# Exchanging the halves of a rotated state by a second matrix product instead of by a transfer, in a State-space and convolution layer

## The chip, the cores and the metric

The kernel runs on one core of a Trainium2 chip. The metric is the device time of one execution in microseconds (us): the median of several executions, and, for everything read from a profile, one profiled execution. The core has five engines that work side by side, each strictly in its own order: TensorE (PE in the profile; its weight loads are listed as PEld), VectorE (DVE), ScalarE (ACT), GpSimd (POOL) and SyncE (SP), which here does nothing but start transfers (DMA).

## The reference

One decoder layer is computed for a prompt of 1024 tokens and for 8 sample tokens that carry on from a stored state, so 1032 columns in all. The model width is 1024. What matters here:

```
xn = rmsnorm(x);  z = xn @ w_in
u, cv, cg = z[:512], z[512:1024], z[1024:1536]; gates = sigmoid(z[1536:])
h_t = a * h_(t-1) + B u_t            # complex, 32 groups of 16 channels, 64 states each
y   = Re(C h) + d * u                # the state-space branch
ya  = (gelu(y) @ w_glu)[:1024] * sigmoid((gelu(y) @ w_glu)[1024:])
c   = silu(layernorm(dwconv31(cv * sigmoid(cg))));  yb = c @ w_pw
x   = x + (gates[:1024] * ya + gates[1024:] * yb) @ w_out
x   = x + (silu(g) * v) @ w_ff_out   # g, v from rmsnorm(x) @ w_ff_in, width 2816
y   = rmsnorm(x)
```

The outputs are y for both groups of tokens, the new complex state and the new rows of the convolution's buffer.

## The kernel before

Channels lie on the 128 partitions and tokens on the free axis. Large products run in fp16 with the weights in two parts (`wh` and `wl`, three products for each block, tile `mm`, L594), 344 or 384 columns at a time; ScalarE and VectorE make the weight parts (L561, L565) with a scale `wsc` (L501) that VectorE computes. The program runs through these stages: load and normalise x and project u (0 to about 92 us in the profile), the products of the convolution's two inputs and of gate a (to about 304), the gated products of the state-space branch (`gyp`, to 437), the layer norm of the convolution (to 448), gate b and the pointwise product (to 538), the output product (to 672), and the feed-forward part (to the end).

The state-space recurrence, called the chain here, lies inside the second stage. It is done in 8 blocks of 4 groups. The 1024 prompt tokens are cut into 128 pieces of 8 tokens, and for each group the 8 x 16 inputs of a piece lie on the 128 partitions, so the tile `U` has 128 columns of pieces for each group, beside 8 columns for the sample tokens. The state lies on the 128 partitions too, 64 real parts above 64 imaginary parts. For each block:

- `s1` (L355): fp32 products `px = E . U` give what each piece adds to the state. ScalarE copies them to `X` in SBUF (L358) and the 8 sample columns to `xs` (L359). Two transfers (L342, L343) write the tile `Y`, which is `X` with its two halves of 64 partitions exchanged, since a rotation needs the real part beside the imaginary part.
- `s2`: VectorE multiplies `X` by cosines (L366) and `Y` by sines (L367), adds them (L368), and runs four scans along the 128 pieces (L371). What is scanned is then real for each row. Two further transfers write the exchanged result back into `X`.
- `s3`: VectorE multiplies by cosine and sine again (L381, L382) and subtracts into `H` (L385), shifted by one piece; `hf` (L386) keeps the last column as the final state. GpSimd sets the first column of `H` and copies the stored state of the sample tokens behind it (L384, L387). TensorE forms `py = Q . H + M . U` (L394, L395), 8 fp32 products of 136 columns. ScalarE and VectorE apply the gelu (L396 to L400), and transfers write `gy` to DRAM (`gd`, L828), from where it is read back as `gyt` with channels on the partitions.

The coefficients are made on the way: `coef_w` makes the matrices `E` (tile `pe`, L301) and, for two blocks together, `kv`; `coef_m` sends `kv` through DRAM (`kvd`, L312) and reads it back as the matrix `M` (L316); `coef_p` makes cosines and sines `pc` for two blocks and spreads them by transfers into `cosi` (L337, L338); `coef_q` makes `Q`. The products `px`, `pe`, `py` and `pf` share one pool of PSUM with two buffers (tag `ms`), so a third of them can start only when the first has been read out.

The loop over t takes 10 steps: step t does `s1` of block t, `s2` of block t-1 and `s3` of block t-2. The order of the instructions on each engine isn't the order of the code: a scheduler simulates the program with its own costs and writes one list for each engine, and `hp()` gives some transfers a higher priority. VectorE also computes the depthwise convolution of 31 taps (L898), which fills its time from about 180 to 430 us, and the statistics of its layer norm: TensorE sums them (`pst`, L1007) and spreads them over the partitions (`prb`, L1021).

Of the kernel before, what the change touches and what calls it, by code (L numbers as in the profile page):

```python
# [36 lines left out]
class S5:  # L37
# [207 lines left out]
    def prep_c(self):  # L245
# [39 lines left out]

    def coef_w(self, m):
        nc, V, A, T = self.nc, self.nc.vector, self.nc.scalar, self.nc.tensor
        kv = self.t([P, 8, 16], "^kv", bufs=1)
        for h in range(2):
            b = 2 * m + h  # L290
            gs = slice(4 * b, 4 * b + 4)
            W = self.t([P, 4, 8, 16], "^W", bufs=2)
# [4 lines left out]
            E = self.t([P, 4, P], "^E", bufs=2)
            for q in range(2):
                pe = self.ps.tile([P, 512], F32, name="pe", tag="ms")
                for g in range(2):  # L300
                    T.matmul(pe[:, 144 * g:144 * g + 144], W[:, 2 * q + g], self.IC[:, 2 * q + g],  # L301
                             start=True, stop=True)
# [1 line left out]
                A.copy(E[:, 2 * q:2 * q + 2], pv[:, :, :P])
# [13 lines left out]
    def coef_p(self, m):  # L318
# [12 lines left out]
        pv = pc.rearrange("p s (b i) x y -> p s b (i x y)", i=2)  # L331
        for h in range(2):
            b = 2 * m + h
            t = self.t([P, 2, 4, P], "^cosi", bufs=2)
            for hi_ in range(2):
                d = t[:, :, 2 * hi_:2 * hi_ + 2].rearrange("p s i n -> p s (i n)")
                SY.dma_start(d[0:64], pv[64 * hi_:64 * hi_ + 64, 0:2, h])  # L337
                SY.dma_start(d[64:128], pv[64 * hi_:64 * hi_ + 64, 0:3:2, h])  # L338
            self.cosi[b] = t
# [5 lines left out]
    def s1(self, b, U):  # L345
        A, T = self.nc.scalar, self.nc.tensor
        E = self.E.pop(b)
        Xf = self.t([P, 4, 136], "X", tag="XY", bufs=6)
        Y = self.t([P, 4, 136], "Y", tag="XY", bufs=6)[:, :, :P]
        X = Xf[:, :, :P]  # L350
        self.st[b] = (X, Y, U, Xf)
        for h in range(2):
            px = self.ps.tile([P, 512], F32, name="px", tag="ms")
            for g in range(2):
                T.matmul(px[:, g * 136:g * 136 + 136], E[:, 2 * h + g], U[:, 2 * h + g, 0:136],  # L355
                         start=True, stop=True)
# [1 line left out]
            A.copy(X[:, 2 * h:2 * h + 2], pv[:, :, 8:136])  # L358
            A.copy(self.xs[:, 4 * b + 2 * h:4 * b + 2 * h + 2], pv[:, :, 0:8])  # L359
        self.swap(Y, X)  # L360

    def s2(self, b):
# [3 lines left out]
        V.tensor_tensor(X, X, co, MUL)  # L366
# [5 lines left out]
        self.swap(X, Y)  # L372

    def s3(self, b, gy_dma):
        nc, V, A, T = self.nc, self.nc.vector, self.nc.scalar, self.nc.tensor
# [9 lines left out]
        V.tensor_tensor(H[:, :, 1:128], Y[:, :, 0:127], X[:, :, 0:127], SUB)  # L385
        V.tensor_tensor(self.hf[:, gs], Y[:, :, 127], X[:, :, 127], SUB)  # L386
        nc.gpsimd.tensor_copy(H[:, :, 128:136], self.h0[:, 0, :, gs].rearrange("p s g -> p g s"))  # L387
        gy = self.t([P, 4, 136], "gy", bufs=1)
        Qf = Q.rearrange("p g k c -> p g (k c)")
        for h in range(2):  # L390
            py = self.ps.tile([P, 512], F32, name="py", tag="ms")
            for g in range(2):
                o = py[:, g * 136:g * 136 + 136]
                T.matmul(o, Qf[:, 2 * h + g], H[:, 2 * h + g], start=True, stop=False)  # L394
                T.matmul(o, M[:, 4 * (b % 2) + 2 * h + g], U[:, 2 * h + g, 8:144], start=False, stop=True)  # L395
            A.copy(Xf[:, 2 * h:2 * h + 2].rearrange("p g n -> p (g n)"), py[:, :272])  # L396
# [6 lines left out]
    def finish(self, rep, imp, res, ims):  # L403
        nc, V, A, T = self.nc, self.nc.vector, self.nc.scalar, self.nc.tensor
        ps = self.ps.tile([P, 512], F32, name="pf", tag="ms")
        T.transpose(ps[:G, :P], self.hf, self.ident)
# [1042 lines left out]
```

## Time and profile before

| what | us |
|---|---|
| median of 3 executions | 1368.21 (1366.9 to 1368.58) |
| the profiled execution | 1366.18 |
| its span, from first to last instruction | 1364.1 |
| TensorE busy with products | 1263.1 (93%) |
| VectorE busy | 1036.5 (76%) |
| ScalarE busy | 621.6 (46%) |
| GpSimd busy | 102.8 (8%) |
| mean clock granted to TensorE | 0.975 |

The page of the profile gives busy shares over the whole span, in which the stage of the chain is less than a fifth. So for this change the views with a window count: how busy each engine was in a stretch, who waited for whom there, the chain of work that ended last, and the list of instructions in order of time. In a list, the number in brackets behind an instruction is the idle time of its engine ahead of it, and what ended it; "issue" is a wait for which the profile shows no releaser. In the views by groups, "x64" is a count and the number behind "busy" is the mean time of one instruction in ns; instructions of one engine overlap, so the distance of two starts is shorter than one duration. An fp32 product stands in the list as two records.

### The profile page before, as it was taken

What the parts mean: (1) busy time and instruction counts of PE and PEld (TensorE: products, weight loads), DVE (VectorE), ACT (ScalarE), POOL (GpSimd) and SP (SyncE); (2) the same over time, 40 slices, a digit from 0 to 9 for tenths busy, and PEclk for the clock granted to TensorE, in tenths of its full rate; (3) what the DMA queues carried; (4) which work ended last, traced back from release to release, by engine and by line L of the source; (5) the groups of instructions that cost most, each with busy time, mean ns of one, the idle gap of its engine ahead of it and who ended that gap; (6) DMA issues with size and microseconds to landing.
All of it is one profiled execution on the core that took longest, in us unless ns stands there. A gap on an engine that the chain in (4) does not pass through costs nothing.

```text
span 1364.1 us, 25399 instructions
## 1 busy us (share of the span) xinstructions
PE 1263.1 (93%) x10083; PEld 1001.7 (73%) x10083; DVE 1036.5 (76%) x2402; ACT 621.6 (46%) x1118; POOL 102.8 (8%) x198
## 2 busy tenths in 40 slices
PE   3898797999998999799979999999999999999996
PEld 2776565666666666578658888888888888888884
DVE  5976788989997744768897857776785777678758
ACT  5843433453333545744354534444453544445522
POOL 5000012001110100000000000000000000000100
PEclk9899898999999999999979999999999999999998
DMA  6445665341122123410011121112112111221203
GB/s 190 130 97 120 135 113 119 81 127 50 48 62 63 30 82 98 135 32 1 17 41 46 40 78 48 40 55 68 50 39 78 48 39 55 68 58 32 77 18 125
DMA packets 169632, 96.66 MB, mean 71 GB/s; under 512 B 12927, under 2 KB 165643, under 8 KB 169513
## 3 DMA queue, kind: packets, MB, share of 16 engines
q1 hardware_dynamic: 168109, 92.44, 24.8%
q0 software_dynamic: 896, 1.63, 0.6%
q8 instruction: 79, 1.29, 0.4%
q10 hardware_dynamic: 507, 0.97, 0.3%
q14 instruction: 41, 0.33, 0.1%
HBM read 76.72 MB, written 9.65 MB: 63 GB/s over the span
## 4 chain that ended last, share of the span: by engine, by line
PE 51%; DVE 26%; issue 9%; DMA 8%; ACT 4%; POOL 1%; SPq 1%; DVEq 0%; ACTq 0%; POOLq 0%
PE q L1291 18%; PE q L1370 12%; PE mm L594 10%; PE q L1177 5%; DMA wr<-in_w_ff_in_dram 5%; DVE acc L898 4%; PE pu L734 2%; DVE ws L1249 2%; DVE wl L565 2%; DVE tb L898 1%; DMA Y<-X 1%; POOL sv L521 1%; ACT ws L1248 1%; DVE g L1270 1%; DVE mh L609 1%
## 5 line engine op out<-in xcount | busy, mean ns | idle before, releaser
L1291 PE MATMUL q<-xs,ws 128*128 128x258 f16 (+2 forms) x3696 | 422.6, 275 | 18.7 <-DVE xs L1225 6.7
L1291 PEld LDWEIGHTS <-ws 128*128 128x128 f16 x3696 | 358.4, 98 | 81.7 <-issue 24.6
L594 PEld LDWEIGHTS <-wh 128*128 128x128 f16 x1728 | 169.5, 98 | 86.2 <-issue 5.1
L594 PE MATMUL mm<-xn,wh 128*128 128x344 f16 (+2 forms) x1152 | 203.8, 311 | 1.9 <-ACT ut L746 1.1
L1370 PE MATMUL q<-hp,wh 128*128 128x258 f16 x1280 | 193.5, 272 | 0.0
L521 POOL PARTITION_ALL_REDUCE sv<-wss x110 | 71.0, 646 | 936.0 <-ACT wh L516 510.7
L1370 PEld LDWEIGHTS <-wh 128*128 128x128 f16 x1280 | 124.0, 97 | 18.1
L561 ACT ACTIVATE wh<-wr,wsc 128x512 f16<-128x512 f32 (+1 forms) x76 | 70.0, 922 | 126.9 <-DVE wsc L501 122.6
L1370 PE MATMUL q<-hp,wl 128*128 128x258 f16 x640 | 122.5, 273 | 0.0
L594 PE MATMUL mm<-xn,wl 128*128 128x344 f16 (+2 forms) x576 | 118.0, 312 | 0.0
L594 PEld LDWEIGHTS <-wl 128*128 128x128 f16 x864 | 85.2, 99 | 41.3 <-issue 0.3
L516 ACT ACTIVATE wh<-wr 128x512 bf16<-128x512 f32 (+1 forms) x78 | 65.0, 833 | 107.6 <-PE q L1370 44.6
L516 ACT ACTIVATE junkw<-wr 128x1024 bf16<-128x1024 f32 x52 | 54.8, 1054 | 109.2 <-DMA wr<-in_w_ff_in_dram 101.6
L565 DVE SCALAR_TENSOR_TENSOR wl<-wr,wsc,wh 128x512 f16<-128x512 f32 (+1 forms) x76 | 75.9, 999 | 22.6 <-ACT wh L561 22.4
L1374 DVE SCALAR_TENSOR_TENSOR x<-q,inv,x 128x516 f32<-128x516 f32 x80 | 59.9, 750 | 35.8 <-PE q L1370 35.6
L1177 PE MATMUL q<-mh,wo 128*128 128x258 f16 x672 | 80.0, 275 | 7.5 <-ACT mh L608 4.2
L1249 DVE SCALAR_TENSOR_TENSOR ws<-sw,wsc,ws 128x512 f16<-128x512 f32 x88 | 64.7, 744 | 19.4 <-ACT ws L1248 18.4
L1177 PEld LDWEIGHTS <-wo 128*128 128x128 f16 x672 | 64.3, 96 | 19.9 <-issue 7.6
L1248 ACT ACTIVATE ws<-sw,wsc 128x512 f16<-128x512 f32 x88 | 62.3, 715 | 28.9 <-PE q L1291 28.8
L1370 PEld LDWEIGHTS <-wl 128*128 128x128 f16 x640 | 61.9, 97 | 9.0
L594 PE MATMUL mm<-gyp,wh 128*128 128x344 f16 x384 | 66.6, 309 | 1.4 <-DVE mg L971 0.8
L1249 DVE SCALAR_TENSOR_TENSOR ws<-wr,wsc,ws 128x512 f16<-128x512 f32 x66 | 48.7, 744 | 17.9 <-ACT ws L1248 17.6
(404 smaller groups left out, 1852.8 us busy)
## 6 DMA issues: line engine op xcount, KB each, us to landing
wr<-in_w_ff_in_dram SPq DMA_DIRECT2D x44, 512.0 KB
wr<-in_w_in_dram SPq DMA_DIRECT2D x28, 512.0 KB
wr<-in_w_ff_out_dram SPq DMA_DIRECT2D x44, 256.0 KB
xt<-in_x_prompt_dram SPq DMA_DIRECT2D x8, 512.0 KB
cosi<-pc SPq DMA_DIRECT2D x32, 128.0 KB
wr<-in_w_glu_dram SPq DMA_DIRECT2D x16, 256.0 KB
wr<-in_w_out_dram SPq DMA_DIRECT2D x8, 512.0 KB
xc<-in_x_prompt_dram SPq DMA_DIRECT2D x8, 512.0 KB
```

The source lines that it names most:

```text
L516: A.activation(junk, src, AF.Square, accum_out=o)
L521: GP.partition_all_reduce(v, ss, P, RMAX)
L561: A.mul(hi, raw, s)
L565: V.scalar_tensor_tensor(lo[:, sl], raw[:, sl], s, hi[:, sl], MUL, SUB)
L594: T.matmul(pt[:, c, :b - a], ww[:, k], aa[:, a:b], start=(k == 0 and i == 0), stop=(k == n - 1 and i == 2))
L898: V.scalar_tensor_tensor(o[:, q:], x[:, 0:HT - q], w[q], o[:, q:], MUL, ADD)
L1177: T.matmul(o, wo[m][u][:, k], cset(mh[k][v], j), start=(k == 0 and q == 0), stop=(k == 7 and q == 2))
L1248: A.mul(w[:, 0], src, s)
L1249: V.scalar_tensor_tensor(w[:, 1], src, s, w[:, 0], MUL, SUB)
L1291: T.matmul(o[:, z, :w_], w[:, u, k * P:(k + 1) * P], xs[k][i][:, v, c, a:b], start=(k == 0 and q == 0), stop=(k == 3 and q == 2))
L1370: T.matmul(pt[:, z, :258], w[u][:, k], hid[k][v][:, c0:c0 + 258], start=(k == 0 and q == 0), stop=(k == blocks[b] - 1 and q == 2))
L1374: V.scalar_tensor_tensor(x, pt[:, :, :258], inv, x, MUL, ADD)
```

## The change

The exchange of halves is no longer done by transfers.

- `E` gets 192 columns, the last 64 a repeat of the first 64. The product with columns 0 to 127 gives the added state, and a second product with columns 64 to 191 gives the same with its halves exchanged. `s1` so has 8 products of 128 columns in two PSUM tiles, and no copy to SBUF; `s2` multiplies straight from PSUM.
- The second exchange is moved into a coefficient: `Qs` is `Q` with its halves exchanged, by two transfers for each block. `H` has two parts, the scanned result times cosine and times sine (written by L385 of the new kernel, twice), and `py` is `Q . H[0] + Qs . H[1] + M . U`. The subtraction is gone. ScalarE copies `hf` (two parts now) and the stored state into `H`.
- The sample tokens' part of `E . U` is made by 4 products of 8 columns for each block, beside `py`.
- The final state takes four products in `finish` instead of a transpose.
- `coef_w` works block by block, `coef_c` (the spreading of cosines) is split off and works block by block too, blocks 0 and 1 are prepared ahead of the loop, `U` is loaded one block ahead, and the loop has 9 steps, with `s1` and `s2` of a block in the same step and `s3` one step later.
- The tiles under tag `XY` have 4 buffers instead of 6, those of `U` 3 instead of 4; the sample columns in `U` and `gy` change places with the prompt's.

```diff
     def coef_q(self, b):
         Q = self.t([P, 4, 8, 16], "^Q", bufs=2)
         self.build(Q, self.C[0], self.C[1], self.D1, self.D2, slice(4 * b, 4 * b + 4))
-        self.Q[b] = Q
-
-    def coef_w(self, m):
+        S = self.t([P, 4, 8, 16], "Qs", bufs=1)
+        self.swap(S, Q)
+        self.Q[b] = Q, S
...
+    def coef_w(self, b):
+        m, h = b // 2, b % 2
+        if h == 0:
+            self.kv[m] = self.t([P, 8, 16], "^kv", bufs=1)
+        kv = self.kv[m]
...
+        E = self.t([P, 4, 192], "^E", bufs=2)
...
+            A.copy(E[:, 2 * q:2 * q + 2, :P], pv[:, :, :P])
+            A.copy(E[:, 2 * q:2 * q + 2, P:], pv[:, :, :64])
+            A.copy(kv[:, 4 * h + 2 * q:4 * h + 2 * q + 2], pv[:, :, P:])
+        self.E[b] = E
+        if h == 1:
+            V.tensor_tensor(kv[0:16], kv[0:16], self.dn[:, m * P:(m + 1) * P].rearrange("p (g c) -> p g c", g=8), ADD)
...
+    def coef_c(self, b):
+        SY = self.nc.sync
+        t = self.t([P, 2, 4, P], "^cosi", bufs=2)
+        for hi_ in range(2):
+            d = t[:, :, 2 * hi_:2 * hi_ + 2].rearrange("p s i n -> p s (i n)")
+            SY.dma_start(d[0:64], self.pc[64 * hi_:64 * hi_ + 64, 0:2, b % 2])
+            SY.dma_start(d[64:128], self.pc[64 * hi_:64 * hi_ + 64, 0:3:2, b % 2])
+        self.cosi[b] = t
...
     def s1(self, b, U):
-        A, T = self.nc.scalar, self.nc.tensor
-        E = self.E.pop(b)
-        Xf = self.t([P, 4, 136], "X", tag="XY", bufs=6)
-        Y = self.t([P, 4, 136], "Y", tag="XY", bufs=6)[:, :, :P]
-        X = Xf[:, :, :P]
-        self.st[b] = (X, Y, U, Xf)
-        for h in range(2):
-            px = self.ps.tile([P, 512], F32, name="px", tag="ms")
-            for g in range(2):
-                T.matmul(px[:, g * 136:g * 136 + 136], E[:, 2 * h + g], U[:, 2 * h + g, 0:136],
-                         start=True, stop=True)
-            pv = px[:, :272].rearrange("p (g n) -> p g n", g=2)
-            A.copy(X[:, 2 * h:2 * h + 2], pv[:, :, 8:136])
-            A.copy(self.xs[:, 4 * b + 2 * h:4 * b + 2 * h + 2], pv[:, :, 0:8])
-        self.swap(Y, X)
+        T = self.nc.tensor
+        E = self.E[b]
+        pz = []
+        for c in (0, 64):
+            pt = self.ps.tile([P, 512], F32, name="px", tag="ms")
+            for g in range(4):
+                T.matmul(pt[:, g * P:g * P + P], E[:, g, c:c + P], U[:, g, 8:136], start=True, stop=True)
+            pz.append(pt.rearrange("p (g n) -> p g n", g=4))
+        self.st[b] = (pz, U)
 
     def s2(self, b):
         V = self.nc.vector
-        X, Y = self.st[b][:2]
-        co, si = self.cosi[b][:, 0], self.cosi[b][:, 1]
-        V.tensor_tensor(X, X, co, MUL)
-        V.tensor_tensor(Y, Y, si, MUL)
+        pz, U = self.st[b]
+        X = self.t([P, 4, P], "X", tag="XY", bufs=4)
+        Y = self.t([P, 4, P], "Y", tag="XY", bufs=4)
+        V.tensor_tensor(X, pz[0], self.cosi[b][:, 0], MUL)
+        V.tensor_tensor(Y, pz[1], self.cosi[b][:, 1], MUL)
         V.tensor_tensor(X, X, Y, ADD)
         for g in range(4):
             r8 = self.mag8[:, 4 * b + g:4 * b + g + 1].to_broadcast([P, P])
             V.tensor_tensor_scan(Y[:, g], r8, X[:, g], 0.0, MUL, ADD)
-        self.swap(X, Y)
+        self.st[b] = (Y, U)
 
     def s3(self, b, gy_dma):
         nc, V, A, T = self.nc, self.nc.vector, self.nc.scalar, self.nc.tensor
         gs = slice(4 * b, 4 * b + 4)
-        X, Y, U, Xf = self.st.pop(b)
+        Y, U = self.st.pop(b)
         cosi = self.cosi.pop(b)
-        co, si = cosi[:, 0], cosi[:, 1]
         M, Q = self.M[b // 2], self.Q.pop(b)
-        V.tensor_tensor(Y, Y, co, MUL)
-        V.tensor_tensor(X, X, si, MUL)
-        H = self.t([P, 4, 136], "H", bufs=1)
-        nc.gpsimd.memset(H[:, :, 0:1], 0.0)
-        V.tensor_tensor(H[:, :, 1:128], Y[:, :, 0:127], X[:, :, 0:127], SUB)
-        V.tensor_tensor(self.hf[:, gs], Y[:, :, 127], X[:, :, 127], SUB)
-        nc.gpsimd.tensor_copy(H[:, :, 128:136], self.h0[:, 0, :, gs].rearrange("p s g -> p g s"))
+        E = self.E.pop(b)
+        H = self.t([P, 2, 4, 137], "H", bufs=1)
+        nc.gpsimd.memset(H[:, :, :, 0:9], 0.0)
+        A.copy(H[:, 0, :, 0:8], self.h0[:, 0, :, gs].rearrange("p s g -> p g s"))
+        for q in range(2):
+            V.tensor_tensor(H[:, q, :, 9:137], Y, cosi[:, q], MUL)
+        A.copy(self.hf[:, :, gs], H[:, :, :, 136])
...
         for h in range(2):
             py = self.ps.tile([P, 512], F32, name="py", tag="ms")
             for g in range(2):
                 o = py[:, g * 136:g * 136 + 136]
-                T.matmul(o, Qf[:, 2 * h + g], H[:, 2 * h + g], start=True, stop=False)
-                T.matmul(o, M[:, 4 * (b % 2) + 2 * h + g], U[:, 2 * h + g, 8:144], start=False, stop=True)
+                i = 2 * h + g
+                T.matmul(o, Qf[0][:, i], H[:, 0, i, 0:136], start=True, stop=False)
+                T.matmul(o, Qf[1][:, i], H[:, 1, i, 0:136], start=False, stop=False)
+                T.matmul(o, M[:, 4 * (b % 2) + i], U[:, i, 0:136], start=False, stop=True)
+                T.matmul(py[:, 272 + 8 * g:280 + 8 * g], E[:, i, :P], U[:, i, 136:144], start=True, stop=True)
             A.copy(Xf[:, 2 * h:2 * h + 2].rearrange("p g n -> p (g n)"), py[:, :272])
+            A.copy(self.xs[:, 4 * b + 2 * h:4 * b + 2 * h + 2], py[:, 272:288].rearrange("p (g n) -> p g n", g=2))
...
-        T.transpose(ps[:G, :P], self.hf, self.ident)
-        fo = self.t([G, P], "fo", tag="XY", bufs=6)
+        for q_ in range(2):
+            c = slice(64 * q_, 64 * q_ + 64)
+            T.matmul(ps[:G, c], self.hf[:, 0], self.ident[:, c], start=True, stop=False)
+            T.matmul(ps[:G, c], self.hf[:, 1], self.ident[:, 64 - 64 * q_:128 - 64 * q_], start=False, stop=True)
...
         if c == 3:
             s5.coef_w(0)
+            s5.coef_w(1)
             s5.coef_m(0)
             s5.coef_p(0)
+            s5.coef_c(0)
+            s5.coef_c(1)
...
-        U = s5.bp.tile([P, 4, 144], F32, name=nm("U"), tag="U", bufs=4)
+        U = s5.bp.tile([P, 4, 144], F32, name=nm("U"), tag="U", bufs=3)
...
-    for t in range(10):
+    us = [load_u(0)]
+    for t in range(9):
         if t < 8:
-            s5.s1(t, load_u(t))
-        if t % 2 == 1 and t < 7:
-            s5.coef_w(t // 2 + 1)
-        if 1 <= t < 9:
-            s5.s2(t - 1)
-        if t >= 2:
-            s5.s3(t - 2, gy_dma)
-        if t % 2 == 1 and t < 7:
-            s5.coef_m(t // 2 + 1)
-        if 1 <= t < 9:
-            s5.coef_q(t - 1)
-        if t % 2 == 0 and 2 <= t < 8:
-            s5.coef_p(t // 2)
+            if t < 7:
+                us.append(load_u(t + 1))
+            s5.s1(t, us[t])
+            s5.s2(t)
+        if t >= 1:
+            s5.s3(t - 1, gy_dma)
+        if t < 8:
+            s5.coef_q(t)
+        if 1 <= t < 7:
+            s5.coef_w(t + 1)
+            if t % 2 == 0:
+                s5.coef_m(t // 2)
+            else:
+                s5.coef_p(t // 2 + 1)
+            s5.coef_c(t + 1)
```

The scheduler writes a new order for all engines. Three places follow, first as before, then as changed. The first is on TensorE, where the result of block 0 is formed (`mm` is the convolution's input product, `xn` its input, `wh` and `wl` the weight parts).

```order
L594 LDWEIGHTS wl_2211
L594 MATMUL mm_2225<-xn_104,wl_2211 128x344
L594 LDWEIGHTS wh_2210
L594 MATMUL mm_2225<-xn_105,wh_2210 128x344
L394 MATMUL py<-H,Q 128x136
L395 MATMUL py<-U_1313,M 128x136
```

```order
L601 MATMUL mm_2219<-xn_105,wl_2205 128x264
L601 LDWEIGHTS wh_2204
L601 MATMUL mm_2219<-xn_106,wh_2204 128x384
L395 MATMUL py<-H,Q 128x136
L396 MATMUL py<-H,Qs 128x136
L397 MATMUL py<-U_1317,M 128x136
L398 MATMUL py<-U_1317,E 128x8
```

The pair of products for each of the 4 groups has become a group of four, and it stands earlier in the order, among the products of `mm_2219`: in the old order the 8 `pe` products of two later blocks and a third set of `px` stood ahead of it, now only the first two sets of 8 `px`.

The second is on SyncE, which starts the transfers, where the matrix `M` of blocks 2 and 3 is fetched.

```order
L342 DMA X<-Y 64x4x128
L343 DMA X<-Y 64x4x128
L312 DMA kvd<-kv 8x128x16
L342 DMA Y<-X 64x4x128
L343 DMA Y<-X 64x4x128
L316 DMA M<-kvd 128x8x128
L337 DMA cosi<-pc 64x2x256
```

```order
L838 DMA gd<-gy 8x16x128 x3
L492 DMA wr_2968<-in_w_in_dram 128x8x128
L838 DMA gd<-gy 8x16x128
L839 DMA gds<-gy 16x4x8
L316 DMA kvd<-kv 8x128x16
L320 DMA M<-kvd 128x8x128
L347 DMA Qs<-Q 64x512
L847 DMA U_1669<-ud_70 128x4x128
```

The four exchanges around the fetch are gone. The write of `kv` and the read of `M` now stand next to each other, behind the transfers of a result `gy`, and `U` of a later block and `Qs` behind them. On TensorE, 13.0 us of products by the distances of the list (with 2.36 columns per ns for `mm`) now lie between the last `pe` of block 3 and the first product with this `M`; 15.2 and 14.2 us in the two cases that follow.

The third is on TensorE at the statistics of the layer norm (`lnq` is the square of the convolution's result, `dg` a diagonal matrix of the statistics).

```order
L594 MATMUL mm_4820<-xn_106,wl_4806 128x344
L1007 MATMUL pst_4635<-ones,lnq_4621 128x1 x8
L1007 MATMUL pst_4635<-ones,lnq_4621 8x1
L1021 MATMUL prb_4667<-dg_4665,ones 128x512
L1021 MATMUL prb_4672<-dg_4670,ones 128x512
L1034 MATMUL prb_4677<-d_453_4675,ones 128x8
L594 LDWEIGHTS wh_4897
```

```order
L601 MATMUL mm_4911<-xn_100,wh_4896 128x344
L1020 MATMUL pst_4726<-ones,lnq_4712 128x1 x8
L1020 MATMUL pst_4726<-ones,lnq_4712 8x1
L601 LDWEIGHTS wh_4896
L601 MATMUL mm_4911<-xn_100,wh_4896 128x344
...
L601 MATMUL mm_4911<-xn_105,wl_4897 128x344
L1034 MATMUL prb_4758<-dg_4756,ones 128x512
L601 LDWEIGHTS wl_4897
```

The first sum stands 60 products of 344 columns earlier, and 50 of them lie between the sums and the first spreading, where nothing lay before. On VectorE the last instruction that writes `H` stood behind 36 taps of the convolution, and now stands behind 51.

More of the change, by code (lines that the diff above doesn't have):

```diff
@@ new lines, in coef_w @@
+        m, h = b // 2, b % 2
+        if h == 0:
+            self.kv[m] = self.t([P, 8, 16], "^kv", bufs=1)
+        kv = self.kv[m]
+        gs = slice(4 * b, 4 * b + 4)
+        W = self.t([P, 4, 8, 16], "^W", bufs=2)
+        self.build(W, self.B[0], self.B[1], self.C1, self.C2, gs)
+        W = W.rearrange("p g i c -> p g (i c)")
+        A.copy(self.IC[0:64, :, P:], self.C[0][0:64, gs])
+        A.mul(self.IC[64:128, :, P:], self.C[1][64:128, gs], -1.0)
+        E = self.t([P, 4, 192], "^E", bufs=2)
@@ new lines, in coef_w @@
+        for q in range(2):
+            pe = self.ps.tile([P, 512], F32, name="pe", tag="ms")
+            for g in range(2):
+                T.matmul(pe[:, 144 * g:144 * g + 144], W[:, 2 * q + g], self.IC[:, 2 * q + g],
+                         start=True, stop=True)
+            pv = pe[:, :288].rearrange("p (g n) -> p g n", g=2)
+            A.copy(E[:, 2 * q:2 * q + 2, :P], pv[:, :, :P])
+            A.copy(E[:, 2 * q:2 * q + 2, P:], pv[:, :, :64])
+            A.copy(kv[:, 4 * h + 2 * q:4 * h + 2 * q + 2], pv[:, :, P:])
@@ L330, in coef_p @@
         A.mul(pc[:, 2], pc[:, 1], -1.0)
[L331 to L339, printed above, removed]
+        self.pc = pc.rearrange("p s (b i) x y -> p s b (i x y)", i=2)
+    def coef_c(self, b):
[6 more added lines that the diff above has]
+        self.cosi[b] = t
     def swap(self, dst, src):
@@ L376, in s3 @@
         gs = slice(4 * b, 4 * b + 4)
-        X, Y, U, Xf = self.st.pop(b)
+        Y, U = self.st.pop(b)
         cosi = self.cosi.pop(b)
-        co, si = cosi[:, 0], cosi[:, 1]
         M, Q = self.M[b // 2], self.Q.pop(b)
-        V.tensor_tensor(Y, Y, co, MUL)
-        V.tensor_tensor(X, X, si, MUL)
-        H = self.t([P, 4, 136], "H", bufs=1)
-        nc.gpsimd.memset(H[:, :, 0:1], 0.0)
-        V.tensor_tensor(H[:, :, 1:128], Y[:, :, 0:127], X[:, :, 0:127], SUB)
-        V.tensor_tensor(self.hf[:, gs], Y[:, :, 127], X[:, :, 127], SUB)
-        nc.gpsimd.tensor_copy(H[:, :, 128:136], self.h0[:, 0, :, gs].rearrange("p s g -> p g s"))
+        E = self.E.pop(b)
+        H = self.t([P, 2, 4, 137], "H", bufs=1)
+        nc.gpsimd.memset(H[:, :, :, 0:9], 0.0)
+        A.copy(H[:, 0, :, 0:8], self.h0[:, 0, :, gs].rearrange("p s g -> p g s"))
+        for q in range(2):
+            V.tensor_tensor(H[:, q, :, 9:137], Y, cosi[:, q], MUL)
+        A.copy(self.hf[:, :, gs], H[:, :, :, 136])
         gy = self.t([P, 4, 136], "gy", bufs=1)
-        Qf = Q.rearrange("p g k c -> p g (k c)")
+        Xf = self.t([P, 4, 136], "Xf", tag="XY", bufs=4)
+        Qf = [q.rearrange("p g k c -> p g (k c)") for q in Q]
         for h in range(2):
@@ L410, in finish @@
         nc.sync.dma_start(imp[0, 0], fo[:, 64:128])
[L411 to L412 removed]
+        hn = self.t([P, 8, G], "hn", tag="XY", bufs=4)
+        h2 = self.t([P, 8, G], "h2", tag="XY", bufs=4)
         V.tensor_tensor(hn, self.h0[:, 0], self.er.to_broadcast([P, 8, G]), MUL)
```

36 lines of the change are left out of this document (7 added, 29 removed).

## The prediction

> **What bounds the kernel now.** I read the page first, for the engines' shares over the whole span, then the stretches of the chain's stage.
>
> ```profile
> PE 1263.1 (93%) x10083; PEld 1001.7 (73%) x10083; DVE 1036.5 (76%) x2402; ACT 621.6 (46%) x1118; POOL 102.8 (8%) x198
> 110.00:259.00 149.00, 127.48 (x867) 94.62 (x868) 123.19 (x248) 54.67 (x137) 19.67 (x36) 0.94 0.53 113
> 259.00:304.00 45.00, 44.27 (x293) 29.25 (x292) 39.31 (x75) 22.80 (x33) 3.05 (x6) 0.96 0.47 127
> 304.00:437.00 133.00, 129.77 (x882) 86.45 (x879) 127.48 (x224) 51.88 (x65) 15.53 (x15) 1.00 0.19 54
> 437.00:449.00 12.00, 8.14 (x30) 5.25 (x31) 5.86 (x24) 4.04 (x5) 0.62 (x1) 0.57 0.15 44
> ```
>
> After the window stand its length and the busy us of PE, PEld, DVE, ACT and POOL (each with its count), then the granted clock. TensorE is the bound nearly everywhere. Only in two stretches does it idle and lose clock: while the chain runs (110 to 259, 127.5 busy of 149, clock 0.94), and at the layer norm (8.1 of 12, clock 0.57). From 304 to 437 TensorE and VectorE are both full (129.8 and 127.5 of 133), so each of them is late if the chain's stage leaves it late. The waits between 90 and 450 us say what ends the idle time (total, times, longest):
>
> ```profile
> PE py L394 <- issue: 7.9, 1, 7.9
> PE py L394 <- DVE H L385: 6.9, 2, 6.3
> PE prb L1021 <- DVE dg L1017: 3.4, 1, 3.4
> PE px L355 <- DMA U<-uds: 3.3, 1, 3.3
> PE pe L301 <- DVE W L279: 2.8, 2, 2.5
> PE pst L1007 <- DVE lnq L1051: 1.7, 1, 1.7
> PE pf L406 <- ACT X L396: 1.6, 1, 1.6
> PE py L394 <- DVE hf L386: 1.0, 2, 0.6
> DVE X L366 <- DMA Y<-X: 17.4, 4, 6.1
> ACT wh L561 <- DVE wsc L501: 34.0, 9, 13.0
> 158.83 1.15 ACT L561 ACTIVATE wh<-wr,wsc 128x1024 f16<-128x1024 f32 x1 [13.04 <-DVE wsc L501]
> 160.40 0.35 ACT L304 COPY E<-pe 128x256 f32<-128x256 f32 x1
> ```
>
> VectorE waits 17.4 us for the first exchange. What stands behind it in VectorE's order waits too, among it the scale `wsc`, for which ScalarE stands still for 13.04 us. The `pe` tiles, which hold both PSUM buffers, are copied only at 160.40, so `py` starts at 160.94 after 7.93 us without a releaser. This reading of "issue" is inferred from the order of the copies. The exchange is therefore a cause of most of TensorE's idle time, though two engines away from it.
>
> **The change part by part.** First what TensorE gains in work. Prices are distances of starts:
>
> ```profile
> 133.00 0.40 PE L394 MATMUL py<-H,Q 128*128 128x136 f32 x2
> 133.23 0.40 PE L395 MATMUL py<-U,M 128*128 128x136 f32 x2
> 161.98 0.66 PE L394 MATMUL py<-H,Q 128*128 128x136 f32 x2
> 162.43 0.66 PE L395 MATMUL py<-U,M 128*128 128x136 f32 x2
> 301.13 1.04 PE L594 MATMUL mm<-xn,wh 128*128 128x344 f16 x6
> 302.44 1.04 PE L594 MATMUL mm<-xn,wh 128*128 128x344 f16 x6
> 437.47 3.17 PE L1007 MATMUL pst<-ones,lnq 128*128 128x1 f32 x18 [1.74 <-DVE lnq L1051]
> 444.03 3.75 PE L1021 MATMUL prb<-dg,ones 128*128 128x512 f32 x4 [3.39 <-DVE dg L1017]
> 447.71 0.59 PE L1034 MATMUL prb<-d,ones 8*128 8x8 f32 x2
> 448.23 1.07 PE L594 MATMUL mm<-xn,wh 128*128 128x344 f16 x6
> ```
>
> An fp32 product of 136 columns costs 0.233 us at full clock and 0.45 right after the long wait, which is half clock. Nine `mm` products take 1.31 us, 0.146 each.
>
> - `px`: 32 products at 0.233 = 7.5 us become 64 of 128 columns, 0.233 x 128/136 = 0.219 each, 14.0 us: +6.6.
> - `Qs . H`: 32 more at 0.233: +7.5.
> - 32 products of 8 columns. The trace has none at full clock in a row. If columns alone counted, one would cost 0.233 x 8/136 = 0.014, 0.4 us in all. The nearest row is `pst`, 9 products of one column in 3.17 us at a clock of 0.57, so 3.17 x 0.57 / 9 = 0.2 at full clock: 6.4 us. I take 6.4, since that row is a short fp32 product with a weight load of its own, and keep 0.4 for the range.
> - `finish`: three products more, +0.3 at most.
>
> Together **+20.8 us** (14.8 by the low price).
>
> [...]
>
> Now what goes from VectorE and its neighbours:
>
> ```profile
> L385 DVE TENSOR_TENSOR H<-Y,X 128x508 f32<-128x508 f32 x8 | 5.4, 676 | 0.0
> L386 DVE TENSOR_TENSOR hf<-Y,X 128x4 f32<-128x4 f32 x8 | 1.3, 162 | 0.0
> L366 DVE TENSOR_TENSOR X<-X,cosi 128x512 f32<-128x512 f32 x8 | 5.5, 686 | 17.4 <-DMA Y<-X 17.4
> L358 ACT COPY X<-px 128x256 f32<-128x256 f32 x16 | 5.8, 370 | 9.0 <-PE px L355 4.7 <-DVE gy L400 4.2
> L304 ACT COPY E<-pe 128x256 f32<-128x256 f32 x14 | 5.1, 370 | 6.0 <-PE pe L301 5.7
> L928 DVE TENSOR_TENSOR pr<-psc,cw x4: 391/404/405, 320.4 to 329.5; 128x240 f32<-128x240 f32 x4
> L413 DVE TENSOR_TENSOR hn<-h,er x1: 417/417/417, 261.9 to 261.9; 128x256 f32<-128x256 f32 x1
> ```
>
> VectorE loses L385 and L386, 5.4 + 1.3 = 6.7 us. Its multiplications from PSUM I price like those from SBUF: 404 ns for 240 elements from PSUM stand beside 417 for 256 from SBUF. [...] ScalarE loses the copies of `X` (5.8 us) and gains as many half-size copies into `E`, and those of `H` and `hf`: even, on an engine busy 55 of 149 us. 32 transfers go from SyncE's queue and 16 (`Qs`) come, off the rotation. The GpSimd copy of the stored state moves to ScalarE.
>
> Next what TensorE stops losing between 110 and 304. The waits of that stretch are 7.9 + 6.9 + 2.8 + 1.6 + 1.0 and five under 0.8, about 23 us; the 3.3 for `U` stands ahead of the first `px` and stays. Clock lost: 0.06 x 127.5 + 0.04 x 44.3 = 9.4 us by the windows, or 8 x (0.45 - 0.233) = 1.7 for each of three or four stalls, 6; I take 8.5. So 31.5 us are lost in all, and without any loss the added 20.8 still leave **10.7 us** gain at 304.
>
> New waits eat into it. `M` is now fetched one block ahead of its use, not a whole pass of the loop:
>
> ```profile
> 100.34 7.37 DMA M<-kvd
> 133.81 0.63 SPq L312 DMA_DIRECT2D kvd<-kv  x1
> 137.23 0.62 SPq L316 DMA_DIRECT2D M<-kvd  x1
> ```
>
> Write to read is 3.4 us, the read 7.4; with the copy of `kv` (0.2) and its addition (0.3), and 1.5 to 4 us for the places in the queues of ScalarE, VectorE and SyncE (there behind the results `gy` of the block before), 12.8 to 15.3 us pass from the last `pe` to `M`. The order leaves 13.0, 15.2 and 14.2 us of TensorE's work for it: waits of 0 to 2.3 us each, and where `gy` is late more; I take 4 + 1 + 3 = 8 (bounds 0 and 16). Behind that wait stand `py` of the block, then its buffer, so the next `pe`. `px` holds both PSUM buffers until VectorE, in its order, has multiplied; what is hidden now behind other products costs up to 3 us a block if VectorE is at a weight part just then; I take 2 in all, bound 24. Cold clock after those: 1. Together **11** (bounds 0 and 41), which leaves the start of the `gyp` products where it is: -10.7 + 11 = +0.3.
>
> Last the layer norm. From 437.47 - 1.74 = 435.73 to 448.23 TensorE has 12.5 us, in which its own work at full clock is 9 x 0.2 + 2 x 0.233 x 512/136 + 0.2 = 3.8. The rest, **8.7 us**, is waiting and half clock. In the new order `pst` stands 60 products, 8.8 us, earlier, and 50 products (7.3 us) cover the 3.39 us wait of `prb`. For that VectorE must be earlier by as much.
>
> ```profile
> 358.03 1.30 DVE acc L898 x2
> ```
>
> A tap of the convolution takes 0.65 us in a row. At the last `H` VectorE has done 51 taps instead of 36, 9.8 us of work more, if the last `H` comes when it came.
>
> So both arrive together, and I take all of it: -8.7. Work after it is the same in the same order.
>
> Sum: +0.3 - 8.7 = **-8.4 us**, 1366.2 - 8.4 = 1357.8 for the profiled execution. The profiled execution lies 2.0 us under the median of the runs, so the median becomes **1360 us**.
>
> **The rivals.**
>
> (a) *The chain loses as much as before.* The lost 31.5 us come back as waits for `M`, for PSUM held by `px`, and for `U` and `Qs` in SyncE's queue. For it: 93% busy TensorE leaves no room, three of the `M` fetches have no spare, and both buffers are held across two engines. Against: the exchange's own waits, the longest of the list, are gone. With waits of 28 us instead of 11 the sum is -10.7 + 28 - 8.7 = +8.6: 1377 us. It turns slower from new waits of 19.4 us on, in particular if the waits of `py` for `M` and of `px` and `pe` for a buffer reach 2.4 us for each of 8 blocks.
>
> (b) *Nearly nothing is lost.* New waits of 1 us, all hidden: -10.7 + 1 - 8.7 = -18.4: 1350 us. For it: VectorE was the root of the waits, and has 17.4 us of them and 6.7 us of work less.
>
> (c) *The layer norm keeps its gap,* because VectorE comes no earlier than TensorE needs it: it is 96% busy from 304 on, and each us that it stands in the chain's stage waiting for `px` is a us later at `lnq`. Then +0.3 remains: 1368.5, no change.
>
> (d) The exchange isn't gone but moved into `Qs`. Those transfers depend on coefficients alone; they'd show as waits of `py` for `Qs`. With one buffer, the next one can start only after `py` has read it. I count this in (a).
>
> **How the numbers follow.** The likeliest case 0.48 (its own range 1354 to 1366), (a) 0.25, (b) 0.14, (c) 0.13. Within 0.2% means 2.7 us of 1368.2, about what a measurement of this kernel can tell from no change: (c) falls there mostly, and the edges of (a) and of the likeliest. Faster 0.61, same 0.14, slower 0.25. The range goes from (b) to (a): 1349 to 1377; the low price of the 8-column products, 6 us less, lies inside it.
>
> **What would show it.** Right: no wait of VectorE for a transfer of `X` or `Y`; TensorE's idle time between 110 and 304 down from 23 to about 10 us, most of it at `py` for `M`; the `gyp` products starting at 304 within 5 us; and no idle time or half clock at `pst` and `prb`. The 8-column products should stand 0.2 us apart from the next. Wrong: idle time at `px` or `pe` behind VectorE of more than 2 us a block, which is (a); `pst` waiting for `lnq`, which is (c); or a stretch after the layer norm that isn't as long as before, since I moved nothing there.

## The result, and the profile after

The changed kernel takes 1376.96 us (median of 5 executions, 1372.74 to 1380.0) against 1366.9 before (5 executions beside them): ratio 1.0075, 95% interval 1.0058 to 1.0091. It is slower by about 10 us, where 8 us faster were forecast. The profiled execution has a span of 1375.0 us against 1364.1.

First the stretches of both kernels, cut at the same events: first `px`, first product with `gyp`, first sum of the layer norm (`pst`), first product behind gate b, end. Columns as in the prediction (length, busy us of PE, PEld, DVE, ACT, POOL, then PE's clock). Before:

```profile
0.00:110.10 110.10, 81.00 (x596) 64.60 (x597) 79.97 (x339) 65.05 (x126) 21.57 (x54) 0.97 0.52 139
110.10:303.75 193.65, 171.50 (x1157) 123.64 (x1158) 162.25 (x321) 77.12 (x169) 22.62 (x40) 0.95 0.52 117
303.75:437.47 133.72, 130.03 (x885) 86.65 (x882) 128.14 (x224) 52.13 (x65) 16.00 (x15) 1.00 0.18 54
437.47:538.02 100.55, 97.11 (x639) 64.74 (x639) 54.40 (x111) 49.88 (x65) 9.49 (x14) 0.95 0.22 64
538.02:1364.00 825.98, 783.45 (x6810) 662.09 (x6810) 611.70 (x1408) 377.40 (x696) 33.16 (x77) 0.98 0.18 55
```

After:

```profile
0.00:113.82 113.82, 79.97 (x601) 63.65 (x601) 78.20 (x337) 63.00 (x129) 21.02 (x54) 0.98 0.50 135
113.82:322.00 208.18, 195.95 (x1351) 150.17 (x1352) 171.00 (x322) 80.88 (x182) 14.61 (x32) 0.94 0.38 97
322.00:446.02 124.02, 120.58 (x824) 81.04 (x822) 117.42 (x207) 48.53 (x61) 15.88 (x14) 1.00 0.18 53
446.02:548.48 102.46, 102.46 (x701) 68.61 (x699) 55.21 (x113) 51.29 (x67) 7.08 (x14) 1.00 0.25 72
548.48:1375.00 826.52, 783.89 (x6811) 661.95 (x6810) 612.01 (x1411) 378.49 (x696) 32.73 (x77) 0.98 0.18 55
```

The five lengths differ by +3.7, +14.5, -9.7, +1.9 and +0.5 us, 10.9 in all. So the chain's stage and its start lose 18.2, the layer norm gives 7.8 back (the third and fourth row belong together, since products moved across the `pst`), and behind gate b next to nothing changes.

The chain's stage can be taken apart further. Cut into stretches of 1 us, each gives an idle time (length less busy), a loss by the clock (busy times one less the clock), and the work that is left, in us at full clock. Summed from the first `px` to the first `gyp` product:

| kernel | first px at | length | idle | lost by clock | work |
|---|---|---|---|---|---|
| before | 110.1 | 193.7 | 22.2 | 7.3 | 164.2 |
| changed | 113.8 | 208.2 | 12.2 | 13.0 | 183.0 |

The work is up by 18.8 us. The idle time did fall by 10, but the clock took back 5.7 of that. What is left of the idle time in this stage has a single main cause, the waits for `M` (waits from 90 to 460 us; the other three lines lie ahead of the first `px` or behind the first `gyp` product):

```profile
PE py L397 <- DMA M<-kvd: 11.6, 3, 4.7
PE px L357 <- DMA U<-ud: 4.8, 1, 4.8
PE mm L601 <- ACT ysg L980: 2.7, 1, 2.7
PE mm L601 <- ACT ut L753: 2.1, 1, 2.1
```

The list of TensorE's instructions around the first of the three waits, and then four stretches around it, show both halves of the loss: the wait, and the slow products behind it.

```profile
162.94 0.60 PE L601 MATMUL mm<-xn,wh 128*128 128x344 f16 x3
168.20 0.82 PE L397 MATMUL py<-U,M 128*128 128x136 f32 x2 [4.66 <-DMA M<-kvd]
168.81 0.43 PE L398 MATMUL py<-U,E 128*128 128x8 f32 x2
```

```profile
164.00:167.00 3.00, 0.00 (x0) 0.00 (x0) 2.84 (x8) 0.22 (x1) 0.00 (x0) 1.00 0.61 103
168.00:170.00 2.00, 1.80 (x8) 1.80 (x9) 0.00 (x0) 0.00 (x0) 0.00 (x0) 0.50 0.03 8
172.00:174.00 2.00, 2.00 (x10) 1.81 (x11) 1.40 (x4) 1.09 (x3) 0.35 (x3) 0.50 0.00 0
175.00:177.00 2.00, 2.00 (x17) 1.50 (x15) 2.00 (x3) 0.53 (x4) 0.00 (x0) 1.00 0.70 181
```

TensorE waits 4.66 us and then works without a gap, but at clock 0.50 (the last column but two), until past 174; from 175 it has 1.00 again. TensorE's last `pe` and SyncE's list tell why `M` is late:

```profile
149.84 0.65 PE L304 MATMUL pe<-IC,W 128*128 128x144 f32 x4
```

```profile
153.02 1.90 SPq L838 DMA_DIRECT2D gd<-gy  x3
155.46 0.58 SPq L838 DMA_DIRECT2D gd<-gy  x1
156.58 0.58 SPq L316 DMA_DIRECT2D kvd<-kv  x1
160.75 0.60 SPq L320 DMA_DIRECT2D M<-kvd  x1
```

The last `pe` of block 3 starts at 149.84, `kv` is written only at 156.58, behind the result `gy` of block 1, the read is issued 4.2 us later, and lands 7.4 us after that, at 168.2. From the last `pe` to `M` pass some 18 us; the order holds 13.0 us of work for it. The sum with `dn` that completes `kv` had ended at 152.8, so 3.8 us of the 18 are the write's place in the queue. For the other two fetches 18.5 and 19.2 us pass (from 196.51 to 215.02 and from 240.77 to 259.94); in the first of them `gy` stands between the write and the read, which are issued 5.4 us apart.

The layer norm went as forecast: no idle time and full clock in the fourth row, and `pst` and `prb` stand between products:

```profile
445.58 0.60 PE L601 MATMUL mm<-xn,wh 128*128 128x344 f16 x3
446.02 1.97 PE L1020 MATMUL pst<-ones,lnq 128*128 128x1 f32 x18
447.92 0.61 PE L601 MATMUL mm<-xn,wh 128*128 128x344 f16 x3
455.22 1.02 PE L1034 MATMUL prb<-dg,ones 128*128 128x512 f32 x2
```

### The profile page after: what moved, and what is told of

It is laid out like the page before. It is cut to its first block, busy times and chain, and to the rows that moved or that the text cites. A ratio compares the mean times of both kernels' runs of the same rounds, so it can differ in the third digit from the quotient of the medians.

```text
span 1375.0 us, 25731 instructions
## 1 busy us (share of the span) xinstructions
PE 1282.8 (93%) x10282; PEld 1025.4 (75%) x10282; DVE 1033.8 (75%) x2386; ACT 622.2 (45%) x1134; POOL 91.3 (7%) x190
## 4 chain that ended last, share of the span: by engine, by line
PE 50%; DVE 18%; issue 13%; DMA 10%; ACT 5%; POOL 1%; SPq 1%; ACTq 0%; DVEq 0%; POOLq 0%
PE q L1304 17%; PE q L1383 15%; PE mm L601 6%; PE q L1190 5%; DMA wr<-in_w_ff_in_dram 5%; DMA M<-kvd 2%; PE pu L741 2%; DVE ws L1262 2%; DVE acc L911 1%; POOL sv L528 1%; ACT mh L615 1%; DVE wl L572 1%; ACT junkw L523 1%; ACT ws L1261 1%; DVE g L1283 1%
## 5 line engine op out<-in xcount | busy, mean ns | idle before, releaser
L601 PE MATMUL mm<-xn,wh 128*128 128x344 f16 (+2 forms) x1152 | 206.7, 312 | 5.5 <-ACT ysg L980 2.7
L528 POOL PARTITION_ALL_REDUCE sv<-wss x110 | 66.0, 601 | 925.9 <-ACT wh L523 500.3
```

Of the source, the lines that this page charges most:

```text
L528: GP.partition_all_reduce(v, ss, P, RMAX)
L601: T.matmul(pt[:, c, :b - a], ww[:, k], aa[:, a:b], start=(k == 0 and i == 0), stop=(k == n - 1 and i == 2))
```

## The experiments

The theory after this reading: TensorE has 18 us more work, and `M`, fetched a block too late, costs its waits and the half clock behind them; the exchange by transfer itself is well removed. The rival: the added work and VectorE's order bound the stage, and the wait for `M` only stands in front of another. Times beside each other come from the same chip; the ratio is to the kernel before, with its 95% interval.

**M a block earlier (m_early).** The buffers of `E` don't allow a third block, so the 8-column products move into the `pe` tiles, where they free `E` in time.

```diff
...
+        if t < 6:
+            s5.coef_w(t + 2, us[t])
+            if t % 2 == 1:
+                s5.coef_m(t // 2 + 1)
         if 1 <= t < 7:
-            s5.coef_w(t + 1)
-            if t % 2 == 0:
-                s5.coef_m(t // 2)
-            else:
+            if t % 2 == 1:
                 s5.coef_p(t // 2 + 1)
```

> The changed kernel with M, E and kv made one block earlier: coef_w two blocks ahead, coef_m at the odd steps, and the 8-column products of blocks 0 to 5 moved into the pe tiles so that E's buffer comes free in time. The work is the same. Theory (waits for M and the half clock behind them): the three waits of py for M (11.6 us in the changed kernel) and three half-clock phases of 6.8 us (3.4 us lost in each) go, 22 us: 1377 - 22 = 1355, range 1350 to 1361, under the kernel before. Rival (TensorE's added work and VectorE's order bound the stage; the wait for M only stood in front of another): py then waits for H or px for its PSUM buffer, and the time stays at 1370 to 1377.

Measured: 1356.87 us, ratio 0.9949 (0.9926 to 0.9971). The waits for `M` are gone and no other of their size took their place:

```profile
PE py L403 <- DMA Qs<-Q: 2.4, 1, 2.4
PE px L364 <- DMA U<-ud: 2.2, 1, 2.2
PE mm L610 <- ACT ysg L990: 1.6, 1, 1.6
```

The stretch of the chain's stage:

```profile
112.90:298.80 185.90, 183.49 (x1348) 140.31 (x1349) 171.02 (x325) 80.45 (x181) 18.73 (x32) 0.99 0.45 109
```

From first `px` to first `gyp` product the stage takes 185.9 us instead of 208.2: 9.8 us less idle, 11.3 less lost by the clock (1.7 instead of 13.0), the work nearly the same (181.8). The half-clock phases behind the waits for `M` had lost 10.0 us in this stage and the one behind the wait for `U` 3.1. The wait for `U` is shorter here (2.2 us instead of 4.8) and no such phase follows it; the one behind the wait for `Qs` loses 1.7. The theory's 22 us came in full between the two profiles (spans of 1375.0 and 1352.2), of which this kernel's is the fastest of its 7 executions; by the two ratios the gain is 17 us. The rival falls.

**The changed kernel again (after_again).**

> The changed kernel once more, unchanged, for a second profile beside these. 1373 to 1380; the waits of py for M 10 to 13 us in all, each followed by half clock that lasts a whole number of 3.4 us periods.

Measured: 1374.88 us, ratio 1.0071 (1.0054 to 1.0088). `M` is waited for 10.9 us in this profile, and the stage loses 11.6 us idle and 8.7 by the clock, against 12.2 and 13.0 in the first one. The waits repeat; what the clock adds differs from one execution to the next. The expectation that each wait is followed by half clock missed: behind the second one, of 1.74 us, the clock stayed full.

**U ahead of M at the start (u_first),** on top of m_early.

```diff
-            s5.coef_m(0)
             s5.coef_p(0)
...
     us = [load_u(0)]
+    s5.coef_m(0)
```

> The kernel with M a block earlier, and M of blocks 0 and 1 fetched after the loads of the first U instead of ahead of them in SyncE's queue. Theory (the 512 KB read of M delays the write and the load of U, which the first px waits for): the wait of px for U of 2 to 5 us goes and px starts near 109.5 us instead of 113: 1357 - 3 = 1354. Rival (U is late because of ScalarE's copy of u, or M is now late for the first py): no change, 1356 to 1360.

Measured: 1352.12 us, ratio 0.9901 (0.9887 to 0.9916). The first `px` starts at 108.42 instead of 112.89 (and 113.82 in the changed kernel):

```profile
108.42 2.05 PE L364 MATMUL px<-U,E 128*128 128x128 f32 x16 [0.97 <-DMA U<-ud]
```

The first load of `U` is issued at 104.77 instead of 109.84, so the fetch of `M` ahead of it in SyncE's queue did delay the start. What is won there doesn't stay whole: the stage is 5.6 us longer (191.5), with 4.2 us idle and 3.3 lost by the clock, the `gyp` products start 1.2 us later than in m_early, and the profiled span is 2.0 us shorter. The medians of the two comparisons differ by 4.8 us. This is the fastest version, 12.3 us under the kernel before by the medians of this comparison (1364.38 to 1352.12).

**Without the 8-column products (no_small),** in the changed kernel:

```diff
-                T.matmul(py[:, 272 + 8 * g:280 + 8 * g], E[:, i, :P], U[:, i, 136:144], start=True, stop=True)
...
-            A.copy(self.xs[:, 4 * b + 2 * h:4 * b + 2 * h + 2], py[:, 272:288].rearrange("p (g n) -> p g n", g=2))
```

> The changed kernel without the 32 products of 8 columns and the copies of their result; the sample tokens' share of the new state is left out (zeros stand in its place). Price by the trace of the changed kernel: a group of four takes 0.92 us against 0.69 for three of 136 columns, so 0.23 each, 7.4 us: 1369.5. If these short products also hold TensorE's clock at half for a second 3.4 us after each wait for M, the half-clock phases shrink from 6.8 to 3.4 us, and 5 us more go: 1364. [...]

Measured: 1365.69 us, ratio 1.0014 (1.0000 to 1.0028), 8 us under the changed kernel by the two ratios. The work of the stage falls by 6.4 us (183.0 to 176.6), 0.20 us for each product. The price from the trace holds; a price by columns alone, 0.4 us in all by the prediction's estimate, falls. The half-clock phases in this profile lasted 3.4, 6.8, 3.4 and 3.4 us where the changed kernel's lasted 6.8 four times, which could mean that short products hold the clock low. The next run speaks against it.

**The same products 112 columns wide (wide_small).**

```diff
-                T.matmul(py[:, 272 + 8 * g:280 + 8 * g], E[:, i, :P], U[:, i, 136:144], start=True, stop=True)
+                T.matmul(py[:, 272 + 112 * g:384 + 112 * g], E[:, i, :P], U[:, i, 32:144], start=True, stop=True)
...
```

> The changed kernel with the 32 products of 8 columns widened to 112 columns, of which the same 8 are copied out. By the price from the trace an 8-column product costs 0.23 us, as much as one of 136; then the widening costs nothing on TensorE and the time stays at 1377, or falls to 1372 if the short products were what held TensorE's clock at half for a second 3.4 us after each wait for M (phases of 6.8 us become 3.4). Rival (columns count, or the 8-column product costs 0.14 as the distance to the next start says): 32 x 0.05 to 0.18 = 2 to 6 us more, 1379 to 1383, and phases of 6.8 us as before.

Measured: 1376.69 us, ratio 1.0088 (1.0069 to 1.0107). An 8-column fp32 product costs as much as one of 112. From one group of four to the next it takes 0.92 us with 112 columns (first products at 123.84 and 124.75) and 0.92 with 8 in the changed kernel (126.85 and 127.77), where three products of 136 take 0.70. The last group of the block:

```profile
126.15 0.39 PE L397 MATMUL py<-U,M 128*128 128x136 f32 x2
126.38 0.37 PE L398 MATMUL py<-U,E 128*128 128x112 f32 x2
126.59 0.71 PE L601 MATMUL mm<-xn,wh 128*128 128x264 f16 x4
```

In the profiled execution the stage lost only 3.8 us by the clock and is 8.0 us shorter than the changed kernel's, but behind gate b this profile is 7.3 us longer, and the median is that of the changed kernel. So nothing can be made of the phases of single profiles. Whether short products matter for the clock stays open.

**Without them and with M early (early_no_small),** m_early with the same lines left out.

> The kernel with M a block earlier, without its 32 products of 8 columns and the copies of their result; the sample tokens' share of the new state is left out. That kernel idles only 2.4 us between the first px and the gyp products. Theory (TensorE is the bound there, so work counts one for one): 32 x 0.23 = 7.4 us less, 1357 - 7.4 = 1349.5. Rival (VectorE is the bound now that M is early, and TensorE's work lies under it): 1355 to 1357.

Measured: 1358.01 us, ratio 0.9941 (0.9924 to 0.9959), no faster than m_early. Here the theory falls: with `M` in time TensorE's work no longer shows one for one. The stage's work is 4.5 us less (177.3) and its length 2.8 less. But in this profile the first `px` starts 2.6 us later, the idle time of the next stage is 2 us more, and the part behind gate b, where the edit changes no line, takes 4.4 us more. What takes the place of the saved work isn't one wait that the profile names, and stays open. The rival, that VectorE is the bound, isn't shown either: TensorE's waits for VectorE in the stage sum to 1.5 us.

**Only the first half of the change (px_only):** both products with `E`, but the second exchange by transfer.

```diff
-        self.st[b] = (Y, U)
+        self.swap(X, Y)
+        self.st[b] = (X, Y, U)
...
-        for q in range(2):
-            V.tensor_tensor(H[:, q, :, 9:137], Y, cosi[:, q], MUL)
+        V.tensor_tensor(Y, Y, cosi[:, 0], MUL)
+        V.tensor_tensor(X, X, cosi[:, 1], MUL)
+        V.tensor_tensor(H[:, :, 9:137], Y, X, SUB)
```

> Only the first half of the change: second product with the widened E and multiplication from PSUM, but the second exchange by transfer, subtraction into H and one product Q.H as before; coefficients block by block as in the change. Theory (work plus waits for M): 7.5 us of products less, 5.4 us more on VectorE, the waits for M stay, so 1369 to 1372. Rival (the exchange by transfer is what costs): py waits 2.5 to 6 us a block for the transfer and its neighbours, 1380 or more.

Measured: 1369.63 us, ratio 1.0034 (1.0018 to 1.0050), as the theory had it; 9.3 us of waits of `py` for `M`.

**The first half with M early (px_early),** the two edits together.

> Only the first half of the change (second exchange by transfer, subtraction, one product Q.H), with M a block earlier. Theory (waits for M with their half clock are the loss in both variants): the run with only the first half idled 9.3 us for M and lost 6.6 us of clock in the chain's stage; both go, 1369.6 - 15 = 1354.5, range 1350 to 1360. Rival (with M in time the second exchange shows as waits of py for H): 1362 to 1370.

Measured: 1366.03 us, ratio 1.0001 (0.9986 to 1.0016). The rival's time is right: with `M` in time the stage still loses 9.4 us idle and 9.1 by the clock, where m_early loses 2.4 and 1.7. VectorE waits for the second exchange. Of TensorE's waits, 3.1 us are at `py` for `H`, as the rival said, and 4.4 at `px` for a PSUM buffer that holds `pe`; what makes that copy late wasn't followed.

```profile
DVE Y L390 <- DMA X<-Y: 7.5, 3, 5.1
PE px L362 <- ACT kv L314: 4.4, 1, 4.4
PE py L402 <- DVE H L392: 3.1, 1, 3.1
```

**Only the second half (q_only):** the first exchange by transfer, the second through `Qs`, coefficients by pairs as before, loop of 9 steps.

```diff
     def s1(self, b, U):
...
+            A.copy(X[:, 2 * h:2 * h + 2], pv[:, :, 0:128])
+        self.swap(Y, X)
...
-        V.tensor_tensor(X, pz[0], self.cosi[b][:, 0], MUL)
-        V.tensor_tensor(Y, pz[1], self.cosi[b][:, 1], MUL)
+        V.tensor_tensor(X, X, self.cosi[b][:, 0], MUL)
+        V.tensor_tensor(Y, Y, self.cosi[b][:, 1], MUL)
```

> Only the second half of the change: first exchange by transfer and copies to SBUF as before, the second through Qs and a two-part H; coefficients by pairs as before, two blocks ahead, 9 steps. TensorE's list has 8.1 us more work than before up to the end of the pointwise product (the whole change has 22). Theory (the sum of work and of losses decides): with the losses of before in the chain's stage, and without the gap at the layer norm (8.7 us), 1366.9 + 8.1 - 8.7 = 1366; with the waits on the exchange hidden by the order, down to 1345. Rival (the first exchange by transfer is what makes VectorE late): the waits of before return in full and the gap at the layer norm too, 1375.

Measured: 1371.46 us, ratio 1.0063 (1.0043 to 1.0083), between the two. The longest wait was a new one, of `py` for `Qs`, whose transfer stands behind the read of `M`:

```profile
PE py L395 <- DMA Qs<-Q: 20.3, 3, 8.6
```

**The same with Qs ahead of M (q_only_2).**

```diff
-        if t % 2 == 1 and t < 7:
-            s5.coef_w(t // 2 + 1)
         if t >= 1:
             s5.s2(t - 1)
             s5.s3(t - 1, gy_dma)
-        if t % 2 == 1 and t < 7:
-            s5.coef_m(t // 2 + 1)
         if t < 8:
             s5.coef_q(t)
+        if t % 2 == 1 and t < 7:
+            s5.coef_w(t // 2 + 1)
+            s5.coef_m(t // 2 + 1)
```

> The kernel with only the second exchange replaced, with Q and Qs made before the matrices of the next pair in each step, so that in SyncE's queue the transfers of Qs for block 1 stand ahead of the read of M. In the version before this three waits of py for Qs took 20.3 us and three of its half-clock phases followed from them. Theory (Qs was late because it stood behind the 512 KB read of M in one queue): most of the 20 us and some 5 us of half clock go, 1371 - 25 = 1346, range 1342 to 1356. Rival (the exchange by transfer makes VectorE late, Qs only stood in front): the wait returns as py for H, 1365 to 1371.

Measured: 1373.02 us, ratio 1.0055 (1.0040 to 1.0070). The rival's mechanism is right, and the time lies 2 us above its range: the wait for `Qs` is gone, and the idle time of the stage is 22.2 us instead of 20.6. VectorE waits for the first exchange, and TensorE for VectorE:

```profile
DVE X L366 <- DMA Y<-X: 21.2, 3, 10.4
PE py L394 <- DVE H L384: 10.4, 2, 5.8
PE py L394 <- DVE Q L279: 8.7, 1, 8.7
```

One thing is mixed into the totals. Behind gate b, where no edit changes a line, the profiles of wide_small, early_no_small, px_early and q_only take 831.6 to 833.8 us, and those of all other kernels 825.8 to 827.8; why isn't shown. So these four totals lie 4 to 8 us higher than the part up to gate b alone would put them. For q_only this is more than its whole distance to the kernel before: up to gate b it takes 536.8 us against 538.0. Against m_early's 525.0 us up to there, px_early (533.4), q_only and q_only_2 (545.4) are still later by 8 us and more.

So an exchange that stays a transfer is waited for in each of these versions, and with both replaced and `M` early the stage runs nearly without waits (2.4 us idle in m_early, 4.2 with `U` first).

## Why the prediction was wrong

The forecast was 1360 us, range 1349 to 1377, and a faster kernel. The median lies at the upper end of the range, on the other side of no change. Rival (a) gave 1377, and the new losses come near its 28 us (25.2). But that its number fits is in part luck: of the waits it named, those for `M` came and the one for `U` grew by 1.5 us, while none came for `Qs`, and `px` waited for VectorE nowhere. Half of the new losses is the clock, which it didn't name.

- *Added work on TensorE, +20.8.* Measured +18.8 in the chain's stage. The price of the 8-column products was right at its order (0.2 forecast, 0.20 to 0.22 measured; the low price fell). In all, no_small measured 6.4 us, as forecast.
- *Lost before, 31.5.* Measured 29.5 (22.2 idle, 7.3 by the clock).
- *New losses, 11.* This is the step that failed: measured 25.2. The idle part of it was nearly right: 10 forecast, 12.2 measured. Waits for `M` are 8 in the forecast and 11.6 measured, since 18 to 19 us passed from the last `pe` to `M` instead of 12.8 to 15.3, with the transfers of `gy` in SyncE's queue ahead of the write or the read. "I take 2 in all" for the PSUM buffers held by `px` came as 0.6 of other waits, none of them at `px` or `pe`. The term that was mis-sized most is "Cold clock after those: 1", measured 13.0 in one profile and 8.7 in the other. I had seen that 1.7 us are lost behind a stall, and used it for the stalls that go, but not for those that come. Four stalls at that price would have been 7, and the forecast near no change; measured behind the three waits for `M` were 3.3 each.
- *The wait for `U` stays.* It grew from 3.3 to 4.8 us, and the chain began 3.7 us later. u_first, where it begins 4.5 us earlier than in m_early, shows that the fetch of `M` ahead of `U` costs that much. But in the kernel before it stood ahead of `U` too (issued at 100.34). The loads of `U` follow it there at 105.77 and in the changed kernel at 109.96, with three transfers of cosines behind the read of `M` that stood elsewhere before; what made the difference wasn't tested.
- *Layer norm, -8.7.* Measured -7.8 over the two stretches. The mechanism was right: `pst` earlier, products up to `prb`, VectorE in time.
- *VectorE's multiplications from PSUM at the price of those from SBUF.* Right:

```profile
L366 DVE TENSOR_TENSOR X<-px,cosi 128x512 f32<-128x512 f32 x8 | 5.4, 679 | 0.0
L368 DVE TENSOR_TENSOR X<-X,Y 128x512 f32<-128x512 f32 x8 | 5.5, 682 | 0.1
```

679 ns from PSUM beside 682 from SBUF.

With the measured parts, the sum is 18.8 + 25.2 - 29.5 + 3.7 - 7.8 + 0.5 = 10.9, as between the two spans.

That the exchange was the cause of most of the old waits fits q_only_2 and px_early, where the one that stays a transfer is waited for again. What the change took with it, the fetch of `M` a block later, undid the gain: by m_early it was worth 17 us by the ratios, 22 in the stage of the profiles.

## What to carry to other kernels

A stall of the engine that bounds the kernel can cost more than its length: here three waits of 2.6 to 4.7 us lost 3.3 us each by the clock behind them. Count the half-clock stretch behind each new wait as you count it for the waits that go. When a change shortens a software pipeline, look at what else was scheduled by the old length, above all transfers through DRAM with a write, a read and a queue in between, and move them a step earlier along with it. And replacing one of two serial exchanges showed no gain here while the other one, or a coefficient, was late: such edits have to be judged together.

## What the runs showed of the hardware that was not expected

The half-clock phases have lengths of whole multiples of 3.4 us. Read off in stretches of 0.4 us, those between 106 and 330 us lasted 3.4, 6.8, 6.8 and 3.4 us before, four times 6.8 in the first profile of the changed kernel, and 3.4, 10.2 and 6.8 in the second. One of them followed a wait of only 2.64 us:

```profile
215.02 0.50 PE L397 MATMUL py<-U,M 128*128 128x136 f32 x2 [2.64 <-DMA M<-kvd]
```

So a wait shorter than the shortest phase can be followed by one; what sets the length of a phase isn't shown. Not every such wait is followed by one. In the changed kernel's first profile the later three of the four phases begin 54.6, 102.4 and 146.8 us behind the first, which is 16, 30 and 43 times 3.41: the phases lie on one grid. In no_small a wait of 2.33 us for `M` (249.85 to 252.18) lies almost whole in one cell (3.41 us) of that profile's grid, and the clock (the last column but two) is at half in the next one. In wide_small a wait of 2.81 us (208.87 to 211.68) lies across two cells, and the clock stays full:

```profile
250.21:253.62 3.41, 1.44 (x12) 1.45 (x13) 2.31 (x6) 0.21 (x1) 0.00 (x0) 1.00 0.41 87
253.62:257.03 3.41, 3.41 (x15) 2.25 (x15) 2.62 (x4) 2.40 (x6) 0.16 (x1) 0.50 0.34 79
```

```profile
207.06:210.47 3.41, 1.80 (x13) 0.98 (x10) 3.41 (x9) 1.15 (x1) 0.00 (x0) 1.00 0.61 107
210.47:213.88 3.41, 2.20 (x19) 2.21 (x20) 2.83 (x5) 0.46 (x2) 0.00 (x0) 1.00 0.01 1
213.88:217.30 3.42, 3.42 (x28) 2.71 (x27) 3.26 (x6) 2.76 (x7) 0.67 (x4) 1.00 0.44 114
```

So the length of a wait doesn't decide alone, and where it falls on the grid may be why what the clock adds differs from one execution to the next; no run varied that by itself. In most of the phases longer than 3.4 us the first cell still holds a part of the wait (0.47 us of the one that ends at 168.20, and 1.53 in the phase of 10.2 us). But behind the wait of 2.64 us two cells pass at half clock in which TensorE is busy without a gap; the cause of the second one stays open.

The other surprise is that an fp32 product of 8 columns costs 0.20 to 0.22 us of TensorE's time, as much as one of 112 and nearly as much as one of 136 (0.23).
